# Spreading the matrix memory's output norm from four rows instead of twelve columns

## The chip, the cores and the metric

The kernel runs on one core of one Trainium2 chip. TensorE multiplies (PE in the profile, its weight loads PEld), VectorE (DVE) and ScalarE (ACT) do the elementwise work, GpSimd (POOL) starts some DMAs and does a little arithmetic, and SyncE (SP) starts the weight loads. The metric is the device time of one execution in microseconds. The kernel before takes 1542.36 us, the median of three runs that lie between 1541.53 and 1542.65 us.

## The reference, cut to what matters

One layer of a hybrid decoder is computed for a prompt of 256 tokens and 8 single-token samples, 264 tokens in all. Two groups of heads share one input projection, and their outputs go side by side into one output projection:

```
xn = rmsnorm(x, g_mix)
z = xn @ w_in
h_rg = RG-LRU scan;  y_rg = rmsnorm(h_rg * gelu(z[rg gate]), g_rg_out)         # 1024 channels
num = ...                                                                     # (token, 4 heads, 256)
den = maximum(abs(den), exp(-m_t));  h = num / den
h_ml = rmsnorm(h, g_ml_out)                                                   # per head, over 256
y_ml = h_ml * sigmoid(z[output gate])                                         # 1024 channels
x = x + concatenate([y_rg, y_ml]) @ w_out
x = x + cross_attention(rmsnorm(x));  x = x + swiglu(rmsnorm(x));  y = rmsnorm(x, g_final)
```

The change is about the factor of `h_ml`: one number for each of 264 tokens and 4 heads, which multiplies the 256 channels of that head. It joins the division by `den` and the norm's inverse root.

## The kernel before, in words

Activations lie transposed: 128 channels on the partitions, 264 tokens along the row. A matrix product is a sequence of *steps*, one for each block of 128 output channels, and a step is a run of up to 16 *chunks* of 128 input channels. To keep float32 precision, weights and activations are split into a high and a low half, and each chunk takes three products of one pass each (`mm3`, in the profile `mm<-B,W`); so a step of 16 chunks is 48 products. The steps touched here are, in this order, the eight RG gate blocks (25 to 32), the eight output-gate blocks (33 to 40, called o0 to o7 below), and the sixteen blocks of `w_out` (41 to 56, called out0, out1, ...). SyncE loads the weights (`raw`); for each half block ACT makes the high half and DVE the low half (`W<-raw`, `W<-raw,W`). A step's result is taken out of PSUM one step later ("evacuated"), on DVE first: for o0 to o7 it is multiplied by `rstd` into a temporary (`t<-mm,rstd`), goes through a sigmoid on ACT, is multiplied by the normed memory output (`t<-t,B`) and is split into the high and low half that `w_out` reads.

Beside the steps run *side works*, Python generators that are advanced after each step. The order in which all of it stands on each engine is not the order in which the code is written: a planner places every instruction by a timeline of its own when the kernel is built, and it is fixed from then on. Every engine takes its instructions strictly in that order.

Three pieces matter.

- `ml_norm` (line 850), the one that is changed. It sums the squares of each head over its 256 channels with `sums` (three products against a column of ones in each head, `ax<-ones,B`, for three blocks of 128 tokens; the third holds the 8 samples). The sums stand as 12 columns, 4 heads by 3 token blocks. DVE makes of them the 12 columns `f`, by an inverse root with three Newton steps (`c<-c`). `spread` (line 359) then turns a column back into a row that is the same on all partitions: the column, repeated 128 times, is the stationary operand, and the identity moves through. It takes three float32 products in each head (128, 128 and 8 columns), and each float32 product is two instructions on PE. DVE multiplies the head's two blocks by the row in PSUM (`B<-B,ax`).
- `later` and `drip` (lines 282 and 287): `sums` of one head are pinned behind a chunk of the running step. With `after=3` the next head's sums come four chunks later, with `after=1` two chunks later; the first head has 1 in both.
- `rg_out` (line 585) makes the RG group's half of what `w_out` reads. Its inverse root is `rstd_wide` (line 384): two one-pass products against ones (`ax<-B,ones_r`) and then twelve DVE instructions over the whole row, each of which needs the one before (`B<-ax`, `B<-B`, `lt<-B`, and three times `B<-lt`, `B<-B`, `lt<-B,lt`). With its result, the tile `lt`, DVE multiplies the eight blocks (`B<-B,lt`), and ACT and DVE split each into high and low (`B<-B,vecs` on ACT, `B<-B,vecs,B` on DVE). The first eight chunks of every `w_out` step read these blocks (`ry`, line 1037), so out0 cannot begin without the first.

```
def ry(c):
    return st["yrg"](c) if c < 8 else st["yml"](c - 8)
```

Buffers of the kind `B` are 26, handed out in turn; PSUM has four banks for the steps (`mm`) and four for all else (`ax`). `ident_r` is a 4 by 4 identity in the one-pass type, and is already used before for two products in each head that spread four rows (line 709: `sel = ident_r[:, h: h + 1].to_broadcast([4, P])`).

Of the kernel before, what the change touches and what calls it, by code (L numbers as in the profile page):

```python
# [10 lines left out]
F32 = mybir.dt.float32  # L11
F32R = mybir.dt.float32r
I32 = mybir.dt.int32
AF = mybir.ActivationFunctionType
# [3 lines left out]
P = 128  # L18
D = 2048
KC = D // P  # L20
T = 256
NS = 8
N = T + NS
# [67 lines left out]
def layer_kernel(ctx: ExitStack, tc, xT, memT, vec, wrg, w_in, w_out, w_q, w_k, w_v, w_o,  # L91
# [3 lines left out]
    act, dve, pe = Engine(nc.scalar, price_act), Engine(nc.vector, price_dve), Engine(nc.tensor, price_pe)  # L95
# [10 lines left out]
    def nm(s):  # L106
        uid[0] += 1
        return f"{s}_{uid[0]}"

    def view(t, shape, skip=0):  # L110
        v = t[:, skip: skip + int(np.prod(shape[1:]))]
        if len(shape) == 2:
            return v
        names = "abcd"[:len(shape) - 1]
        return v.rearrange(f"p ({' '.join(names)}) -> p {' '.join(names)}",
                           **{c: int(n) for c, n in zip(names[1:], shape[2:])})

    def B(shape, dt=F32, skip=0):
        return view(sb.tile([P, SLOT], dt, tag="B", bufs=NB, name=nm("B")), shape, skip)
# [162 lines left out]
    def later(*fs, after=0):  # L282
        k = [after, list(fs)]
        drips.append(k)
        return k
# [13 lines left out]
    def bank(tag="mm"):  # L299
        return psm.tile([P, 512], F32, tag=tag, bufs=4, name=nm(tag))  # L300
# [4 lines left out]
    ident = const.tile([P, P], F32, name="ident")  # L305
# [5 lines left out]
    ident_r = const.tile([4, H], F32R, name="ident_r")  # L311
# [20 lines left out]
    def ctile(w):  # L332
        t = sb.tile([P, 16], F32, tag="c", bufs=8, name=nm("c"))
        return t[:, :w]

    def rsqrt(v, y):

        w = v.shape[-1]
        i = ctile(w).bitcast(I32)
        dve.tensor_single_scalar(i, v.bitcast(I32), 1, op=OP.logical_shift_right)  # L340
        dve.tensor_scalar(y.bitcast(I32), i, -1.0, 1597463007.0, op0=OP.mult, op1=OP.add)
        t = ctile(w)
        for _ in range(3):
            dve.tensor_mul(t, y, y)
            dve.scalar_tensor_tensor(t, t, -0.5, v, op0=OP.mult, op1=OP.mult)
            dve.scalar_tensor_tensor(y, t, 1.5, y, op0=OP.add, op1=OP.mult)
# [5 lines left out]
    def token_sums(ps, acc, o=0, step=1):  # L352

        for j, w0 in enumerate(WIN if acc.shape[-1] == N else WIN[:2]):
            i = pe.matmul(ps[:, o + j * step: o + j * step + 1], acc[:, w0: w0 + P], ones[:, 0:1],
                          start=True, stop=True)
        return i

    def spread(ps, c, n=N):

        for j in range(2 if n == T else 3):
            lo, hi = (j * P, j * P + P) if j < 2 else (T, N)
            i = pe.matmul(ps[:, lo:hi], c[j].to_broadcast([P, P]), ident[:, P - (hi - lo):], start=True, stop=True)
        return i
# [39 lines left out]
    def sumsq(acc, x, first):  # L404
        if first:
            return act.activation(acc, x, AF.Square)
        s = tmp(x.shape[-1])
        i = act.activation(s, x, AF.Square)
        dve.tensor_add(acc, acc, s)
        return i  # L410
# [439 lines left out]
    def ml_norm():  # L850

        while not (ml["pg"].done and ml["sg"].done) or st["i"] < 33:
            yield STEP
        hh = hT["t"]
        a = B([P, H, N])
        for h in range(H):
            for vb in range(2):
                act.activation(hh(2 * h + vb)[:, T:N], nums[:, 2 * h + vb, :], AF.Copy)
            sumsq(a[:, h, :], hh(2 * h), True)
            sumsq(a[:, h, :], hh(2 * h + 1), False)  # L860
            yield 0.35
        yield STEP
        ps = bank("ax")
        r, v, f = ctile(12), ctile(12), ctile(12)

        def sums(h):
            i = token_sums(ps, a[:, h, :], 3 * h)
            if h == 0:
                dve.tensor_max(r.rearrange("p (h j) -> p j h", j=3), den.rearrange("p (h j) -> p j h", j=3),
                               emc.rearrange("p (j h) -> p j h", h=H))  # L870
                dve.reciprocal(r, r)
                dve.tensor_mul(v, r, r)
            if h == H - 1:
                dve.scalar_tensor_tensor(v, ps[:, 0:12], 1.0 / 256, v, op0=OP.mult, op1=OP.mult)
                dve.tensor_scalar(v, v, EPS, None, op0=OP.add)
                rsqrt(v, f)
                dve.tensor_mul(f, f, r)
            return i

        for h in range(H):  # L880
            k = later(lambda h=h: sums(h), after=3 if h else 1)
        while k[1]:
            yield STEP
        for h in range(H):
            ps = bank("ax")
            spread(ps, [f[:, 3 * h + j: 3 * h + j + 1] for j in range(3)])
            for vb in range(2):
                dve.tensor_mul(hh(2 * h + vb), hh(2 * h + vb), ps[:, :N])
            yield 0.7
            ml["nn"] = h + 1  # L890
# [511 lines left out]
    for i, (src, cols, pef, evf, need) in enumerate(steps):  # L1402
# [20 lines left out]
        ps = pef(i)  # L1423
# [13 lines left out]
        if i == 24:  # L1437
            ml["ng"] = side(ml_norm(), -1)
# [115 lines left out]
```

## Time and profile before

| what | before |
|---|---|
| median of three runs | 1542.36 us |
| the profiled execution's own time | 1543.04 us |
| its span, first to last instruction | 1541.3 us |
| PE busy | 1528.6 us, 99% of the span |
| DVE busy | 1061.2 us, 69% |
| ACT busy | 782.9 us, 51% |
| chain of work that ended last, share on PE | 98% |

A row of the timeline gives the start in us from the span's start, the length, the engine, the operation, the tiles as out<-in, and the count of instructions that it merges; in brackets stands how long the engine was idle before it and what ended the wait. A row of the chain of waits gives start, length, engine and tile. All instructions that pass the clock-keeping helper carry its line, L63, so they are told apart by their tiles. PE's rows overlap: a product of 264 columns takes some 0.28 us from start to end, while the next one starts 0.12 us after it.

### The profile page before, as it was taken

The page shows a single profiled execution, that of the slowest core. Times are in us where ns is not written, and L with a number is a line of the kernel's source. Part 1 is how long each engine was busy: PE and PEld are TensorE (multiplying, and loading weights), DVE is VectorE, ACT ScalarE, POOL GpSimd, SP SyncE. Part 2 cuts the span into 40 slices and gives each one's busy share as a digit, 9 for nine tenths or more (in the row PEclk, how much of TensorE's full clock was granted, in tenths as well). Part 3 has the DMA queues.
Part 4 walks back from the last instruction along what each step waited for, and adds up shares of the span by engine and source line. Part 5 has one row for each costly group of instructions (what it writes and reads, how often), then busy time and mean ns, then how long its engine had stood idle before and what let it go on. Part 6 is the DMA issues. An engine that isn't in the chain of part 4 may idle for free.

```text
span 1541.3 us, 30024 instructions
## 1 busy us (share of the span) xinstructions
PE 1528.6 (99%) x12056; PEld 1495.3 (97%) x12056; DVE 1061.2 (69%) x2012; ACT 782.9 (51%) x1233; POOL 126.9 (8%) x190
## 2 busy tenths in 40 slices
PE   8999999999999999999999999999999999999997
PEld 8999999999998888899999999999999999999997
DVE  7976887878798989966675555545555554555554
ACT  6455875655555666654444444334444433444463
POOL 0001120000133334310000000000000000000000
PEclk9999999999999999999999999999999999999999
DMA  7655886556789798856555555555555555555563
GB/s 287 198 169 179 300 306 219 183 183 233 258 317 332 258 350 294 273 167 199 179 188 181 183 187 180 187 181 184 186 181 187 181 187 183 181 189 179 164 176 114
DMA packets 92316, 326.00 MB, mean 212 GB/s; under 512 B 10801, under 2 KB 11233, under 8 KB 92177
## 3 DMA queue, kind: packets, MB, share of 16 engines
q1 hardware_dynamic: 76752, 270.40, 52.7%
q0 software_dynamic: 15136, 53.16, 9.7%
q8 instruction: 94, 1.54, 0.4%
q10 hardware_dynamic: 288, 0.53, 0.1%
q14 instruction: 46, 0.37, 0.1%
HBM read 312.78 MB, written 11.28 MB: 210 GB/s over the span
## 4 chain that ended last, share of the span: by engine, by line
PE 98%; DVE 1%; DMA 0%; ACT 0%; issue 0%; ACTq 0%; DVEq 0%
PE mm L63 93%; PE ax L63 5%; DVE B L63 0%; DMA xres<-xT 0%; DVE W L63 0%; ACT B L63 0%; DVE c L63 0%; DVE t L63 0%; ACTq L304 0%; DVE lt L63 0%; DVEq L1531 0%; ACT W L63 0%; ACT c L63 0%; ACT L63 0%; ACTq L63 0%
## 5 line engine op out<-in xcount | busy, mean ns | idle before, releaser
L63 PE MATMUL mm<-B,W 128*128 128x264 f32 (+2 forms) x11008 | 1363.2, 285 | 0.4 <-DVE W L63 0.4
L63 PEld LDWEIGHTS mm<-B,W 128*128 128x128 f32 x11008 | 1340.8, 188 | 12.1 <-DVE W L63 0.6
L63 ACT ACTIVATE W<-raw 128x1024 fp32r<-128x1024 f32 (+2 forms) x520 | 536.7, 1034 | 649.4 <-PE mm L63 445.5
L63 DVE TENSOR_TENSOR W<-raw,W 128x1024 fp32r<-128x1024 f32 (+2 forms) x520 | 620.2, 1195 | 353.7 <-ACT W L63 352.2
L63 PE MATMUL mm<-W,B 128*128 128x512 f32 x384 | 92.4, 395 | 0.0
L63 PEld LDWEIGHTS mm<-W,B 128*128 128x128 f32 x384 | 71.0, 188 | 16.1
L63 DVE TENSOR_TENSOR t<-mm,rstd 128x264 f32<-128x264 f32 x104 | 44.8, 432 | 44.1 <-PE mm L63 43.9
L1446 POOL TENSOR_TENSOR B<-B,rstd 128x264 f32<-128x264 f32 x4 | 2.8, 732 | 854.0 <-ACT rstd L63 854.0
L63 DVE TENSOR_TENSOR xres<-xres,mm 128x264 f32<-128x264 f32 (+1 forms) x81 | 34.2, 425 | 34.8 <-PE mm L63 34.7
L63 DVE SCALAR_TENSOR_TENSOR B<-B,dw 128x256 f32<-128x256 f32 x128 | 53.8, 475 | 1.8 <-ACT dw L63 1.7
L63 DVE SCALAR_TENSOR_TENSOR dw<-B,qsm,dw 128x256 f32<-128x256 f32 x96 | 51.4, 545 | 2.1 <-ACT dw L63 1.7
L63 PE MATMUL ax<-B,B 128*128 128x256 f32 (+3 forms) x288 | 48.2, 308 | 0.0
L1087 POOL TENSOR_TENSOR dr<-dw,dr 128x256 fp32r<-128x256 f32 x32 | 38.6, 1207 | 102.3 <-ACT dr L63 102.2
L63 PEld LDWEIGHTS ax<-B,B 128*128 128x128 f32 x288 | 40.9, 190 | 2.6
L63 ACT ACTIVATE B<-xres,vecs 128x264 fp32r<-128x264 f32 (+1 forms) x64 | 31.0, 502 | 2.0 <-DMA xres<-xT 1.9
L1076 POOL DMA_DIRECT2D B<-kcT x32 | 17.4, 543 | 134.9 <-DVE B L63 126.7
L63 ACT ACTIVATE dw<-B,qsm 128x256 f32<-128x256 f32 x32 | 16.3, 508 | 22.8 <-DVE B L63 8.9
L63 ACT ACTIVATE B<-t 128x264 fp32r<-128x264 f32 (+1 forms) x60 | 24.5, 408 | 4.5 <-DVE t L63 4.5
L63 ACT ACTIVATE t<-t 128x264 f32<-128x264 f32 (+1 forms) x61 | 24.7, 407 | 3.3 <-DVE t L63 3.3
L63 ACT ACTIVATE t<-xres 128x264 f32<-128x264 f32 (+2 forms) x46 | 18.7, 409 | 14.5 <-DVE xres L63 14.5
L63 DVE SCALAR_TENSOR_TENSOR B<-xres,vecs,B 128x264 fp32r<-128x264 f32 x48 | 22.3, 488 | 1.8 <-ACT B L63 1.8
L63 ACT ACTIVATE t<-B,B 128x128 f32<-128x128 f32 x64 | 19.9, 390 | 5.3 <-DMA B<-scr 5.3
(167 smaller groups left out, 657.2 us busy)
## 6 DMA issues: line engine op xcount, KB each, us to landing
raw<-w_gu SPq DMA_DIRECT2D x176, 512.0 KB, 3.6
raw<-w_d SPq DMA_DIRECT2D x80, 512.0 KB, 3.6
raw<-w_in SPq DMA_DIRECT2D x78, 512.0 KB, 4.5
raw<-w_out SPq DMA_DIRECT2D x32, 512.0 KB, 3.9
raw<-w_q SPq DMA_DIRECT2D x32, 512.0 KB, 5.3
B<-kcT POOLq DMA_DIRECT2D x32, 512.0 KB, 8.4
B<-vcT POOLq DMA_DIRECT2D x32, 512.0 KB, 9.7
raw<-w_k SPq DMA_DIRECT2D x32, 512.0 KB, 6.6
```

The costliest lines, as they stand in the source:

```text
L63: return f(*a, **k)
L1076: pool_e.dma_start(kc, kcT[h, b])
L1087: pool_e.tensor_sub(wr[:, 1], acc, wr[:, 0].bitcast(F32))
L1446: e.tensor_mul(st["y"](c), st["y"](c), r)
```

## The change

The twelve columns `f` are first turned into four rows, one for each head, with 264 tokens in a row: three float32 products whose stationary operand is the four heads' column of one token block and through which the identity moves (`turn`). ACT copies the rows as their high half, DVE takes the low half. A head's factor is then spread to all partitions by two one-pass products of 264 columns, whose stationary operand is a column of the 4 by 4 identity repeated 128 times. It takes one more PSUM bank (`fp`) and one more `B` buffer (`hl`). The sums of heads 1 to 3 come two chunks apart, instead of four.

```
+        fp = bank("ax")
+        hl = B([P, 2, N], F32R)[0:4]
+
+        def turn():
+            fj = f.rearrange("p (h j) -> p j h", j=3)
+            for j, w0 in enumerate((0, P, T)):
+                w = min(P, N - w0)
+                pe.matmul(fp[0:4, w0: w0 + w], fj[:, j, :], ident[:, P - w:], start=True, stop=True)
+            act.activation(hl[:, 0], fp[0:4, :N], AF.Copy)
+            dve.tensor_sub(hl[:, 1], fp[0:4, :N], hl[:, 0].bitcast(F32))
+
         for h in range(H):
-            k = later(lambda h=h: sums(h), after=3 if h else 1)
+            k = later(lambda h=h: sums(h), after=1)
         while k[1]:
             yield STEP
+        turn()
         for h in range(H):
             ps = bank("ax")
-            spread(ps, [f[:, 3 * h + j: 3 * h + j + 1] for j in range(3)])
+            sel = ident_r[:, h: h + 1].to_broadcast([4, P])
+            for k in range(2):
+                pe.matmul(ps[:, :N], sel, hl[:, k], start=k == 0, stop=k == 1)
             for vb in range(2):
                 dve.tensor_mul(hh(2 * h + vb), hh(2 * h + vb), ps[:, :N])
             yield 0.7
```

The planner orders the engines anew for this code. Three places are shown as they stand in a row in the two built kernels; the number behind a name is the buffer's.

On PE, where the factor is spread: first before, in step o4 (its bank is mm_3333), where c_3096 is `f` and ax_3192 to ax_3210 are the heads' banks.

```order
L63 MATMUL mm_3333<-B_139,W_3251 128x264
L63 MATMUL ax_3192<-ident,c_3096 128x128 x2
L63 MATMUL ax_3192<-ident,c_3096 128x8
L63 MATMUL ax_3198<-ident,c_3096 128x128 x2
L63 MATMUL ax_3198<-ident,c_3096 128x8
```

Four such groups stand there in one piece, five products into o4. Now the four rows are made (ax_3097) four products before the end of o3 (mm_3260):

```order
L63 MATMUL ax_3097<-ident,c_3096 4x128 x2
L63 MATMUL ax_3097<-ident,c_3096 4x8
L63 MATMUL mm_3260<-B_182,W_3107 128x264 x2
L63 MATMUL mm_3260<-B_183,W_3107 128x264
L63 MATMUL mm_3260<-B_182,W_3107 128x264
```

And they are spread 19 products into o4 (mm_3330); B_3098 holds their halves, and ax_3199 to ax_3214 are the heads' banks:

```order
L63 MATMUL ax_3199<-B_3098,ident_r 128x264
L63 MATMUL ax_3204<-B_3098,ident_r 128x264
L63 MATMUL ax_3209<-B_3098,ident_r 128x264
L63 MATMUL mm_3330<-B_163,W_3254 128x264
L63 MATMUL ax_3199<-B_3098,ident_r 128x264
L63 MATMUL ax_3204<-B_3098,ident_r 128x264
L63 MATMUL ax_3209<-B_3098,ident_r 128x264
L63 MATMUL ax_3214<-B_3098,ident_r 128x264 x2
```

One group of twelve float32 products became a group of three small ones and, 23 step products later, eight one-pass products in two groups. The RG group's two products against ones stood 24 step products into o4 and now stand 43 into it.

On DVE, from the end of the RG group's inverse root on: first before. lt_3097 is its result, t_3535 and t_3600 are the evacuations of o6 (mm_3482) and o7 (mm_3547), B_1699 and B_1704 the RG blocks, B_3312 their low halves.

```order
L63 SCALAR_TENSOR_TENSOR B_3099<-B_3099 128x264
L63 TENSOR_TENSOR t_3535<-mm_3482,rstd 128x264
L63 SCALAR_TENSOR_TENSOR lt_3097<-B_3099,lt_3097 128x264
L63 TENSOR_TENSOR B_1699<-B_1699,lt_3097 128x264 x4
L63 TENSOR_TENSOR W_3544<-raw_3462,W_3544 128x8x128
L63 TENSOR_TENSOR B_1704<-B_1704,lt_3097 128x264 x4
L63 TENSOR_TENSOR t_3535<-t_3535,B_2465 128x264
L63 SCALAR_TENSOR_TENSOR B_3312<-B_1699,vecs,B_3311 128x264 x4
L63 TENSOR_TENSOR W_3606<-raw_3531,W_3606 128x8x128
L63 SCALAR_TENSOR_TENSOR B_3391<-B_1704,vecs,B_3390 128x264 x2
L63 SCALAR_TENSOR_TENSOR B_3402<-t_3397,vecs,B_3401 128x264
L63 TENSOR_TENSOR t_3600<-mm_3547,rstd 128x264
```

And now, where lt_3099 is the result, t_3538 and t_3603 belong to o6 and o7 (mm_3550), and B_3315 is the low half:

```order
L63 SCALAR_TENSOR_TENSOR lt_3099<-B_3101,lt_3099 128x264
L63 TENSOR_TENSOR t_3538<-t_3538,B_2465 128x264
L63 TENSOR_TENSOR B_3101<-lt_3099 128x264
L63 SCALAR_TENSOR_TENSOR B_3101<-B_3101 128x264
L63 TENSOR_TENSOR W_3609<-raw_3531,W_3609 128x8x128
L63 SCALAR_TENSOR_TENSOR lt_3099<-B_3101,lt_3099 128x264
L63 TENSOR_TENSOR t_3603<-mm_3550,rstd 128x264
L63 TENSOR_TENSOR B_1699<-B_1699,lt_3099 128x264 x4
L63 TENSOR_TENSOR B_1704<-B_1704,lt_3099 128x264 x4
L63 TENSOR_TENSOR W_3612<-raw_3533,W_3612 128x8x128
L63 TENSOR_TENSOR t_3603<-t_3603,B_2465 128x264
L63 SCALAR_TENSOR_TENSOR B_3315<-B_1699,vecs,B_3314 128x264 x3
```

Before, the eight blocks are multiplied by the result, and four of them split, ahead of the evacuation of o7. Now the multiplications stand behind it.

On PE, where out0 (mm_3615) and out1 (mm_3688) begin, now; B_3314 and B_3315 are the high and low halves of the first four RG blocks:

```order
L63 MATMUL mm_3550<-B_182,W_3479 128x264
L63 MATMUL mm_3615<-B_3314,W_3544 128x264
L63 MATMUL mm_3688<-B_3314,W_3609 128x264
L63 MATMUL mm_3615<-B_3315,W_3544 128x264
L63 MATMUL mm_3615<-B_3314,W_3544 128x264 x2
L63 MATMUL mm_3688<-B_3315,W_3609 128x264
L63 MATMUL mm_3688<-B_3314,W_3609 128x264 x2
```

Before, the first three rows of out0 and out1 stood in the same order. In both, PE has two products to do with the first high half; the third needs the first low half.

## The prediction

> **What bounds the kernel now.** I read the page first. PE is busy almost throughout, and the chain that ended last runs along PE:
>
> ```profile
> span 1541.3 us, 30024 instructions
> PE 1528.6 (99%) x12056; PEld 1495.3 (97%) x12056; DVE 1061.2 (69%) x2012; ACT 782.9 (51%) x1233; POOL 126.9 (8%) x190
> L63 PE MATMUL mm<-B,W 128*128 128x264 f32 (+2 forms) x11008 | 1363.2, 285 | 0.4 <-DVE W L63 0.4
> ```
>
> So what PE does more or less is time, and so is any wait of PE. In 11008 step products PE waited 0.4 us in all; nothing later in the kernel has slack from which a loss could be repaid: the 12.7 us in which PE is idle lie at the start and behind its last product. Then I read the chain of waits in the stretch from the norm to `w_out`:
>
> ```profile
> 246.82 0.56 PE ax L63 x6
> 247.38 7.20 PE mm L63 x59
> 254.57 2.58 PE ax L63 x24
> 274.98 0.04 DVE B L63
> 279.22 1.70 DVE B L63 x4
> 280.92 1.15 DVE W L63
> 282.11 2.93 PE mm L63 x22
> ```
>
> The spread is 2.6 us of PE's path. But near 279 us the chain leaves PE and runs over DVE: that is the RG group's half of `w_out`'s input, and PE's one wait (0.42 us) stands at its end. Here DVE is just in time, which makes its order the second thing to look at.
>
> **The direct cost on PE.** The timeline of PE gives what is removed, and what a one-pass product costs:
>
> ```profile
> 253.81 0.76 PE L63 MATMUL mm<-B,W 128*128 128x264 f32 x5
> 254.41 2.74 PE L63 MATMUL ax<-ident,c 128*128 128x128 f32 x24
> 257.01 2.52 PE L63 MATMUL mm<-B,W 128*128 128x264 f32 x19
> 259.37 0.41 PE L63 MATMUL ax<-B,ones_r 128*128 128x264 f32 x2
> 259.61 0.64 PE L63 MATMUL mm<-B,W 128*128 128x264 f32 x4
> ```
>
> From start to start the 24 instructions take 257.01 - 254.41 = 2.60 us, 0.108 each; the five before them 0.12 each; the two against ones 0.24. The 19 behind take 2.36 us, 0.08 more than 19 x 0.12: the price of coming back to the steps. What is added has two near relatives:
>
> ```profile
> 126.95 0.47 PE L63 MATMUL ax<-ident,B 4*128 4x4 f32 x5
> 127.29 1.04 PE L63 MATMUL ax<-B,ident 4*128 4x16 f32 x8
> 147.91 0.50 PE L63 MATMUL ax<-B,ident_r 4*128 4x256 f32 x2
> 148.34 0.92 PE L63 MATMUL ax<-B,B 128*128 128x256 f32 x4
> ```
>
> The turn is six instructions. They lie between 0.067 us (0.34 / 5, a result of four partitions and four columns) and 0.108 us (the removed ones, with as many moving columns): 0.40 to 0.65 us; I take 0.55, since four of the six move 128 columns. The eight products are of the third row's kind, two in 0.43 us, 0.215 each, 1.72 us; if they ran like those against ones, at 0.12, 0.96 us. I take 1.72, as the row has the same operand of four partitions. There are three groups in place of one, so two more returns: 0.16 (0 to 0.32). The sum is -2.60 + 0.55 + 1.72 + 0.16 = -0.2 us, with bounds of -1.2 and +0.1. By TensorE: Matmul & The Clock Gate in the Trainium skill, section "Why this matters for your kernels", a product over 32 rows takes as long as one over 128, which would make it 0.12 each and the sum about -0.9; the third row above, at 0.215, does not agree.
>
> **What lies beside.** ACT's copy of four rows and DVE's subtraction (0.4 us each by rows of 264 elements below) stand between the turn and the spread, with 23 step products, 2.8 us, over them. The sums of squares are the same 24 instructions, only closer together; DVE's tiny column work starts earlier. The load queues and POOL issue what they did. A gain in any of this is hidden: what counts is when `w_out` can begin.
>
> **What the new order costs.** DVE takes its rows strictly in order. Before, the inverse root of the RG group ends just behind the evacuation of o6, and everything for out0 lies in the step that follows:
>
> ```profile
> 273.59 0.43 DVE L63 SCALAR_TENSOR_TENSOR B<-B 128x264 f32<-128x264 f32 x1
> 274.18 0.43 DVE L63 TENSOR_TENSOR t<-mm,rstd 128x264 f32<-128x264 f32 x1 [0.16 <-PE mm L63]
> 274.53 0.42 DVE L63 SCALAR_TENSOR_TENSOR lt<-B,lt 128x264 f32<-128x264 f32 x1
> 274.98 1.47 DVE L63 TENSOR_TENSOR B<-B,lt 128x264 f32<-128x264 f32 x4
> 276.37 1.22 DVE L63 TENSOR_TENSOR W<-raw,W 128x1024 fp32r<-128x1024 f32 x1
> 277.50 1.46 DVE L63 TENSOR_TENSOR B<-B,lt 128x264 f32<-128x264 f32 x4
> 278.88 0.43 DVE L63 TENSOR_TENSOR t<-t,B 128x264 f32<-128x264 f32 x1
> 279.22 1.70 DVE L63 SCALAR_TENSOR_TENSOR B<-B,vecs,B 128x264 fp32r<-128x264 f32 x4
> 280.84 1.22 DVE L63 TENSOR_TENSOR W<-raw,W 128x1024 fp32r<-128x1024 f32 x1
> ```
>
> The second row waits for PE: DVE reaches an evacuation before the step is done. In the new order the eight multiplications stand behind the next evacuation, that of o7, which cannot start before PE has done all that precedes `w_out`. The reason is in the order rows: the two products against ones come 19 step products later in o4, so the twelve dependent DVE instructions start behind other work and end one evacuation later.
>
> Let T be the moment at which PE could start out0. A product ends 0.285 us after its start and the next would start 0.12 after it, so the evacuation of o7 starts about T + 0.20. From there, in the new order and with the lengths above from start to start: the evacuation 0.35; eight multiplications at 1.39 / 4, 2.78; the weights' low half 1.13; the multiplication of o7's kind 0.34; the first low half 0.49 to its end. The first low half is there at T + 5.3. The first high half comes from ACT:
>
> ```profile
> 274.23 1.06 ACT L63 ACTIVATE W<-raw 128x1024 fp32r<-128x1024 f32 x1 [1.81 <-PE mm L63]
> 275.19 0.41 ACT L63 ACTIVATE t<-t 128x264 f32<-128x264 f32 x1
> 275.50 1.72 ACT L63 ACTIVATE B<-B,vecs 128x264 fp32r<-128x264 f32 x4
> ```
>
> In the new order the same three kinds follow each other behind o7, so it ends 0.20 + 1.27 + 0.50 after T, at T + 2.0. PE waits 2.0 us, does the two products that need only the high half, waits again until T + 5.3, 3.0 us, and then goes on; the fourth low half stands behind three of the other group, six places of 0.41 us behind the first, T + 7.7, against 17 products, T + 7.3: some 0.3 us more. That is 5.3 us of waiting. It takes the place of the 0.42 us before, which were for the weights of out1, now split ahead of o7's evacuation:
>
> ```profile
> 282.11 2.08 PE L63 MATMUL mm<-B,W 128*128 128x264 f32 x15 [0.42 <-DVE W L63]
> ```
>
> So the wait costs 5.3 - 0.4 = 4.9 us. Bounds: 4.4, if the smaller waits close up and DVE's hand-overs are free, and 5.3.
>
> **The clock behind the wait.** The windows show how PE's speed follows its work:
>
> ```profile
> 9.75:13.05 3.30, 3.30 (x16) 1.00 1.04 405
> 13.20:16.50 3.30, 3.30 (x29) 1.00 1.04 420
> 1532.00:1534.00 2.00, 1.27 (x12) 1.00 0.01 4
> 1534.00:1538.00 4.00, 0.00 (x0) 0.69 0.97 362
> 1538.00:1541.00 3.00, 0.00 (x0) 0.50 0.59 235
> ```
>
> (Columns: window, its length, PE busy and products, granted clock, DMA share, GB/s.) Until 13.1 us a product takes 0.22 us, then 0.12, though the column shows no throttle there. At the end PE has its last work before 1533.3, and the clock is halved at 1535.5, since a mean of 0.69 over 4 us is 1.5 us of full and 2.5 of half. So 2.2 us without work were enough. In the wait above PE works 0.24 us in 5.2, with one idle stretch of 3.0. I expect the clock to be halved there. What that costs is bounded by nothing below and, above, by the start, where PE needed this long at half speed before it got full speed:
>
> ```profile
> 8.00 5.26 PE L63 MATMUL ax<-B,W 128*128 128x264 f32 x20 [2.67 <-ACT B L63]
> 13.06 0.45 PE L63 MATMUL mm<-B,W 128*128 128x264 f32 x2
> ```
>
> That is 5.06 us, of which 1 - 0.12 / 0.22 is lost, 2.3 us. A slower PE also needs the late low halves later, which takes back the 0.3 us: 2.0 us.
>
> **The sum.** -0.2 + 4.9 + 2.0 = +6.7 us. The profiled execution took 1543.04 us with a span of 1541.3, 0.7 us above the median of 1542.36; on the median I predict 1549.1 us.
>
> **The rivals.**
> - *The clock stays up*: the same wait, but two idle stretches of 2.0 and 3.0 us, with work between, do not halve it. For it: at 254 us and elsewhere no such stretch exists, so the only row is that of the end, where the idle time went on. Then +4.7, 1547.1 us. The page named above says in the same section that idle gaps over about 3 us take the clock back, and in Part 1 that it takes a whole idle window of about 3.4 us; by that the clock stays here, and the time is this rival's.
> - *PE finds the halves ready* (the other side): if the RG chain catches up, so that the multiplications wait for nothing but their place, and the first low half is there at T, no wait is left, the 0.42 us goes too, and eight products at 0.12 save 1.2: 1540.7 us. It decides at the evacuation of o7: DVE would have to start it before o7 is done, against the bracket on the row at 274.18.
> - *Only the high half is late*: if the low half came within the 2 us of the first wait, 2.0 - 0.4 - 0.2 = +1.4, 1543.8 us. Against it stand nine DVE instructions between the first multiplication and the first low half, 3.9 us by the rows.
> - *The turn does not do what it says*: eight four-row products at 0.215 are no cheaper than the twelve of float32. This is inside the forecast, as -0.2 us.
>
> **How the numbers follow.** Forecast 0.55; the clock stays up 0.27; ready halves 0.05; only the high half late 0.08; a longer time at half clock, or a second halving, with 1551 us and more, 0.05. The forecast's own range is 1548 to 1550.2. For 8 in 10 the range must take in the second case down to 4.4 - 1.2 - 0, 1545.6 us, and goes up to 1551.0. A change of 0.2%, 3.1 us, is what a measurement of this kernel tells from none. Under 1539.3 I see only the second rival with an unseen gain, 0.02; within 0.2%, up to 1545.4, the two small-wait cases, 0.12; slower 0.86.
>
> **What would show it.** In the changed profile: the spread's eight products at 0.2 us each, and the three groups together about 2.4 us; DVE's row `B<-B,lt` behind the evacuation of o7; two idle stretches on PE's first `w_out` products, 2 and 3 us, released by ACT and by DVE; then about twenty products at 0.22 us and a granted clock of 0.5 for some 3 to 5 us; nothing later that differs. I am wrong if PE's idle time there is under 2 us, or if a difference arises behind 300 us.

## The result and the profile after

The changed kernel takes 1548.56 us, the median of six runs between 1547.83 and 1550.16; the kernel before, beside it, 1542.31 (1541.53 to 1542.65). The ratio is 1.004, with a 95% interval of 1.003 to 1.005: slower by some 6.2 us. The prediction was 1549.1. The profiled execution of the changed kernel took 1547.83 us, the lowest of its six, with a span of 1545.8.

The page of the changed kernel, its engines and the group of all step products:

```profile
span 1545.8 us, 30007 instructions
PE 1529.1 (99%) x12046; PEld 1494.6 (97%) x12046; DVE 1060.5 (69%) x2013; ACT 784.3 (51%) x1234; POOL 126.6 (8%) x190
L63 PE MATMUL mm<-B,W 128*128 128x264 f32 (+2 forms) x11008 | 1365.7, 285 | 4.6 <-DVE B L63 2.6
```

PE has 10 records less, and its step products waited 4.6 us where they had waited 0.4. The timeline of PE has the new groups and, at the end, the two waits:

```profile
245.75 6.27 PE L63 MATMUL mm<-B,W 128*128 128x264 f32 x51
251.94 0.64 PE L63 MATMUL ax<-ident,c 128*4 128x128 f32 x6
252.51 3.02 PE L63 MATMUL mm<-B,W 128*128 128x264 f32 x23
255.46 0.62 PE L63 MATMUL ax<-B,ident_r 4*128 4x264 f32 x3
256.01 0.39 PE L63 MATMUL mm<-B,W 128*128 128x264 f32 x1
256.33 0.87 PE L63 MATMUL ax<-B,ident_r 4*128 4x264 f32 x5
257.13 3.04 PE L63 MATMUL mm<-B,W 128*128 128x264 f32 x23
260.00 0.41 PE L63 MATMUL ax<-B,ones_r 128*128 128x264 f32 x2
260.24 18.01 PE L63 MATMUL mm<-B,W 128*128 128x264 f32 x149
280.17 0.59 PE L63 MATMUL mm<-B,W 128*128 128x264 f32 x2 [1.91 <-ACT B L63]
283.41 16.80 PE L63 MATMUL mm<-B,W 128*128 128x264 f32 x123 [2.65 <-DVE B L63]
```

On DVE the same stretch shows why: the evacuation of o7 comes first, and behind it the eight multiplications, the weights of the next step, one more multiplication, and only then the low halves.

```profile
277.70 0.43 DVE L63 SCALAR_TENSOR_TENSOR lt<-B,lt 128x264 f32<-128x264 f32 x1
278.29 0.43 DVE L63 TENSOR_TENSOR t<-mm,rstd 128x264 f32<-128x264 f32 x1 [0.16 <-PE mm L63]
278.64 2.83 DVE L63 TENSOR_TENSOR B<-B,lt 128x264 f32<-128x264 f32 x8
281.38 1.22 DVE L63 TENSOR_TENSOR W<-raw,W 128x1024 fp32r<-128x1024 f32 x1
282.52 0.43 DVE L63 TENSOR_TENSOR t<-t,B 128x264 f32<-128x264 f32 x1
282.86 1.30 DVE L63 SCALAR_TENSOR_TENSOR B<-B,vecs,B 128x264 fp32r<-128x264 f32 x3
```

On ACT the first high half is the third thing behind o7:

```profile
278.34 1.06 ACT L63 ACTIVATE W<-raw 128x1024 fp32r<-128x1024 f32 x1 [1.81 <-PE mm L63]
279.30 0.41 ACT L63 ACTIVATE t<-t 128x264 f32<-128x264 f32 x1
279.62 1.31 ACT L63 ACTIVATE B<-B,vecs 128x264 fp32r<-128x264 f32 x3
```

The clock, in windows cut where it changes (columns: window, its length, PE busy and products, granted clock, DMA share, GB/s):

```profile
277.03:280.45 3.42, 1.51 (x13) 1.00 0.60 207
280.45:283.86 3.41, 0.76 (x4) 0.50 0.14 42
283.86:287.27 3.41, 3.41 (x17) 0.50 0.37 138
287.27:290.69 3.42, 3.42 (x31) 1.00 0.00 0
```

It was half from 280.45 to 287.27, for 6.83 us. Up to 283.41 of that PE stood mostly in the second wait, which DVE ended and not PE, so this part cost nothing. In the third window PE was busy throughout and did 17 products; in the fourth, 31. The window ahead of the fall holds only the first wait: PE was busy for 1.51 us of it.

Whole times vary by a few us between executions, so a stretch is used in what follows: from the last evacuation before the first sums of squares (left as it was by the change) to a query evacuation in the cross attention. Before, and then after, on DVE:

```profile
239.76 0.43 DVE L63 TENSOR_TENSOR t<-mm,rstd 128x264 f32<-128x264 f32 x1 [0.43 <-PE mm L63]
408.80 0.42 DVE L63 TENSOR_TENSOR B<-mm,rstd 128x256 f32<-128x256 f32 x1 [0.51 <-PE mm L63]
```

```profile
238.31 0.43 DVE L63 TENSOR_TENSOR t<-mm,rstd 128x264 f32<-128x264 f32 x1 [0.43 <-PE mm L63]
413.34 0.42 DVE L63 TENSOR_TENSOR B<-mm,rstd 128x256 f32<-128x256 f32 x1 [0.51 <-PE mm L63]
```

That is 169.04 us before and 175.03 after, 5.99 more. From the second row to the end of the span it is 1132.5 us in both, so nothing later differs. What lies ahead of the first row was 1.45 us shorter in this execution of the changed kernel; that is chance, and the start of the program, where it arises, is shown below.

### The profile page after: what moved, and what is told of

It is laid out like the page before. It is cut to its first block, busy times and chain, and to the rows that moved or that the text cites. A ratio compares the mean times of both kernels' runs of the same rounds, so it can differ in the third digit from the quotient of the medians.

```text
span 1545.8 us, 30007 instructions
## 1 busy us (share of the span) xinstructions
PE 1529.1 (99%) x12046; PEld 1494.6 (97%) x12046; DVE 1060.5 (69%) x2013; ACT 784.3 (51%) x1234; POOL 126.6 (8%) x190
## 4 chain that ended last, share of the span: by engine, by line
PE 99%; DVE 1%; DMA 0%; ACT 0%; issue 0%; ACTq 0%; DVEq 0%
PE mm L63 93%; PE ax L63 5%; DVE B L63 0%; DMA xres<-xT 0%; ACT B L63 0%; DVE W L63 0%; DVE c L63 0%; ACTq L304 0%; DVE t L63 0%; DVEq L1545 0%; ACT W L63 0%; ACT c L63 0%; ACT L63 0%; ACTq L63 0%
```

## The experiments

The theory was this: the change's own work on PE costs next to nothing; the loss is that VectorE's multiplications of the RG blocks got behind the last evacuation, which makes PE wait at out0 and lose its clock. Two questions were put: is it the order of the RG half, or the new spread itself; and does the clock cost time of its own. The table has all versions together (us; the stretch is that of the profiled execution, with the same two rows).

| kernel | median | kernel before beside it | ratio, 95% interval | stretch | PE's waits at out0 |
|---|---|---|---|---|---|
| before | 1542.31 | | | 169.04 | 0.42 |
| the change | 1548.56 | 1542.31 | 1.004, 1.003 to 1.005 | 175.03 | 1.91 + 2.65 |
| the change, RG half two places earlier | 1541.95 | 1542.2 | 0.9998, 0.9989 to 1.0007 | 168.16 | none |
| before, RG half two places earlier | 1543.33 | 1542.2 | 1.0002, 0.9993 to 1.0011 | 168.27 | none |
| before, sums two chunks apart | 1541.92 | 1542.2 | 0.9997, 0.9988 to 1.0006 | 168.33 | none |
| the change, sums four chunks apart | 1549.86 | 1542.1 | 1.005, 1.0038 to 1.0062 | 176.13 | 4.05 + 1.46 |
| the change, 22 products as filler | 1546.71 | 1542.2 | 1.003, 1.002 to 1.0041 | 173.59 | none |
| the change, 9 products | 1548.8 | 1542.1 | 1.0045, 1.0033 to 1.0056 | 174.87 | 2.72 |
| the change, 13 products | 1547.87 | 1542.1 | 1.0038, 1.0025 to 1.0051 | 173.58 | 2.01 |
| the change, 17 products | 1547.27 | 1542.57 | 1.0027, 1.0016 to 1.0038 | 173.59 | 1.12 |
| the change again | 1549.79 | 1542.57 | 1.0048, 1.0034 to 1.0062 | 175.11 | 1.91 + 2.65 |

**The RG half earlier, with the change.**

```
-                st["rgout"] = side(rg_out(), 0)
+                st["rgout"] = side(rg_out(), -2)
```

> The changed kernel with the RG output work moved back by two places of the list, so that VectorE has the eight multiplications of the RG gate behind it before the last output-norm evacuations; the four-row spread is untouched. If the two waits at out0 are all of the loss (the theory): no wait at out0 above 0.2 us, no half clock in the middle, and 1541.3 to 1542.0 us, some 6.5 to 7 us below the changed kernel and level with the kernel before (1542.3) or up to 1 us below it. If the four-row spread itself is what costs (the rival: more PE work, switching between four-row and full products, buffers of the output norm held longer): no better than 1547. If other work that is moved aside by this is late in turn: a new wait of 1 us or more somewhere between o2 and o7.

DVE's timeline has the multiplications early, ahead of the evacuation in the third row and of all that follow:

```profile
250.22 0.77 DVE L63 TENSOR_TENSOR B<-B,lt 128x264 f32<-128x264 f32 x2
250.99 2.15 DVE L63 TENSOR_TENSOR B<-B,lt 128x264 f32<-128x264 f32 x6
255.56 0.42 DVE L63 TENSOR_TENSOR t<-mm,rstd 128x264 f32<-128x264 f32 x1
```

PE doesn't wait at out0, and the granted clock is whole there. The time is 1541.95 us, 6.6 below the changed kernel, with the four-row spread kept. So the spread is not what costs. No new wait of PE shows in the rest of the stretch either. The move does more than bring eight rows forward: the RG group's products against ones now stand between the first sums of squares, at 239.87 us, and the spread follows only at 269.45. Of all versions run this is the one to keep if the spread is wanted; it can't be told from the kernel before (0.9998).

**The same move without the change.** The same line, in the kernel before.

> The kernel before with the same move of the RG output work by two places; the old spread. Theory: only the 0.42 us wait of the kernel before at out0 goes, so 1541.8 to 1542.2 us. Beside the changed kernel with the same move it prices the change's own instructions on PE: the forecast says -0.2 us for the four-row spread; if the spread costs more than it removes, the changed kernel with the move is the slower of the two.

The median, 1543.33, missed the expected 1541.8 to 1542.2, but its interval holds no change. The stretch is sharper: 168.27 against 169.04, so the one wait of 0.42 us was worth 0.77. The starts of single products in the trace of before say where the rest is: where PE took up work again, the distance to the product before is 0.70 us, and to the next 0.225, where 0.12 is usual, 0.69 more in all. Beside the version above, the four-row spread itself is worth 168.16 - 168.27 = -0.11 us. That is hardly more than the 0.08 us by which the two stretches of the changed kernel in the table differ, so it shows that the spread costs nothing rather than what it saves.

**The sums alone.**

```
-            k = later(lambda h=h: sums(h), after=3 if h else 1)
+            k = later(lambda h=h: sums(h), after=1)
```

> The kernel before with one part of the change only: the sums of squares are taken two chunks apart (after=1), the spread is the old one. Theory: the order of VectorE's list at o6 and o7 decides, not the distance of the sums by itself; here the eight RG multiplications stand ahead of the evacuation of o6, so out0 doesn't wait: 1541.5 to 1542.3 us. If the longer distance of the sums is what makes the halves late in the change: a wait at out0 of 2 us or more and 1545 us or longer.

Here the planner put the eight multiplications ahead of o6's evacuation, the second row:

```profile
272.33 2.83 DVE L63 TENSOR_TENSOR B<-B,lt 128x264 f32<-128x264 f32 x8
275.08 0.43 DVE L63 TENSOR_TENSOR t<-mm,rstd 128x264 f32<-128x264 f32 x1
```

PE doesn't wait at out0, and the time is 1541.92 us. The distance of the sums by itself harms nothing.

**The rows alone.** The changed kernel, with the line above put back as it was.

> The changed kernel with the other half of the change undone: four rows and one-pass products stay, the sums of squares are taken four chunks apart as in the kernel before (after=3 for the second output head). The Newton steps of the last heads end later, so VectorE's eight RG multiplications stand even further behind. Theory: the waits at out0 add up to 6.5 to 7.5 us against 4.6 in the changed kernel, and with the half clock behind them the kernel takes 1549.5 to 1551.5 us. If the waits of the changed kernel come from the two-chunk distance: less wait than 4.6 us and 1546 or below.

The time, 1549.86, is in the expected range; the waits are not. They add up to 5.5 us. On DVE:

```profile
278.56 0.43 DVE L63 TENSOR_TENSOR t<-mm,rstd 128x264 f32<-128x264 f32 x1 [0.16 <-PE mm L63]
279.72 1.22 DVE L63 TENSOR_TENSOR W<-raw,W 128x1024 fp32r<-128x1024 f32 x1
280.86 0.42 DVE L63 SCALAR_TENSOR_TENSOR lt<-B,lt 128x264 f32<-128x264 f32 x1
281.55 2.83 DVE L63 TENSOR_TENSOR B<-B,lt 128x264 f32<-128x264 f32 x8
284.29 0.90 DVE L63 SCALAR_TENSOR_TENSOR B<-B,vecs,B 128x264 fp32r<-128x264 f32 x2
```

The multiplications begin 3.0 us behind the evacuation (0.35 in the change), but the weights' split is done ahead of them and not behind, so the first low half comes only some 1.2 us later, and the stretch is 1.1 us longer. So it is the four rows, by the order that the planner then made of the rest, that bring the loss; the closer sums make it a little smaller.

The traces bear out the reason that the prediction gave, the later place of the RG group's two products against ones. From the first row of the stretch to these products it is 17.3 us with the sums alone, 19.6 before, 21.7 in the change and 24.1 with the rows alone; the eight multiplications begin 33.8, 35.2, 40.3 and 43.0 us behind that row. What in the four rows makes the planner place them so (the products' new places, one more PSUM bank, one more buffer) was not tried.

**Filler in the wait.** The clock was tried by giving PE something to do. Products of a constant, whose result nothing uses, stand between o7 and out0. All else is in the order of the changed kernel, but for one pair of rows on DVE and one on ACT that change places some 10 us later, where PE doesn't wait. The edit is cut to its main lines:

```
+            if fill:
+                fb = bank("ax")
+                with tc.issue_after(st["m"].ins):
+                    for _ in range(fill):
+                        g = pe.matmul(fb[:, :P], ones, ones, start=True, stop=True)
...
+             need=("rgout",) if m == 0 else (), fill=22 if m == 0 else 0)
```

> The changed kernel with 22 float32 products of a constant (44 instructions, about 4.75 us at 0.108 us each) put on PE between the last output-norm group and out0; they are computed and not used, everything else stands in the same order. The RG halves come as late as in the changed kernel (T+2.0 and T+5.3), but PE has work while it waits for them. If the order of the late halves and the clock both cost what the forecast says: the waits shrink to about 0.5 us in all, the filler takes their place, no product near the start of the output projection takes 0.22 us, and the kernel takes about 1546.5 to 1547.2 us, 1.4 to 2 us less than the changed kernel's 1548.6. If the half clock is only a label in the records and costs nothing: 1548.6 again. If PE's products can't run beside VectorE's and ScalarE's work on the halves without holding it up: longer than 1549.

```profile
278.54 5.07 PE L63 MATMUL ax<-ones 128*128 128x128 f32 x44
283.37 0.88 PE L63 MATMUL mm<-B,W 128*128 128x264 f32 x3
```

With 4.8 us more of PE work than the changed kernel the time is 1546.71, 1.85 less, and the granted clock stays at 1.00 here. The stretch, 173.59 us, is 1.44 below that of the changed kernel: this is what the half clock costs.

**How much idle time it takes.** The same with 9, 13 and 17 products, and the changed kernel again beside the last.

> As the 22-product filler, but with 9 products (about 1.95 us): they cover the first wait, and the second one, about 2.8 to 3.0 us, stays. PE waits once instead of twice. If one gap of 3 us is enough to halve the clock: products of 0.22 us behind it for 3.4 or 6.8 us, and the same 1548.0 to 1549 as the changed kernel. If it takes the two gaps together (about 4.8 of 5.2 us idle): the clock stays whole and the kernel takes as long as with 22 products, 1546.5 to 1547.2 us.

> As the 22-product filler, but with 13 products (about 2.8 us): one wait of 2.0 to 2.4 us stays ahead of the first low half. If the clock follows the idle time in a window of about 3.4 us, whole windows only: no half clock, 1546.5 to 1547.2 us. If a wait of 2.2 us is enough, as the end of the program in the kernel before suggests: half clock behind it, about 1548 us.

> As the filler before, with 17 products (about 3.7 us): one gap of 1.1 to 1.4 us stays ahead of the first low half. The earlier traces show the clock changing on a grid of 3.41 us, halved after a stretch of the grid in which PE worked 0.44 of the time or less, and kept after one with 0.50 (9, 13 and 0 products of filler: 0.20, none, 0.44). If that is how it goes, a gap this short can take no stretch below 0.58, wherever the grid falls: no half clock in the middle in any execution, and 1546.2 to 1547.2 us, as with 22 products, without the times of 1547.7 to 1548.9 that four of the five executions with 13 products took. If any wait at out0 brings the half clock with it: 1548 again.

> The changed kernel itself, beside the 17-product filler on one chip: both theories have it at 1548 to 1549.5 us, with half clock behind out0 in every execution, because its two gaps (5.15 us with 0.25 us of work between them) always leave at least one stretch of the 3.41 us grid nearly empty. It gives the price of the half clock without a difference between chips: 1.4 to 2.0 us by the trace (16 products at 0.22 instead of 0.12 us, less what the gap lost anyway); under 0.5 us if the records of the clock mean nothing for the time.

The windows lie again on the grid on which the clock changes in each trace. With 9 products:

```profile
277.28:280.70 3.42, 3.42 (x31) 1.00 0.61 201
280.70:284.11 3.41, 0.69 (x5) 1.00 0.14 46
284.11:287.52 3.41, 3.41 (x18) 0.50 0.37 138
287.52:290.93 3.41, 3.41 (x30) 1.00 0.02 5
```

With 13, where the gap of 2.0 us was split between two windows:

```profile
278.71:282.13 3.42, 3.11 (x28) 1.00 0.48 158
282.13:285.54 3.41, 1.71 (x14) 1.00 0.44 147
285.54:288.95 3.41, 3.41 (x29) 1.00 0.04 14
```

With 17:

```profile
278.97:282.39 3.42, 2.30 (x20) 1.00 0.18 48
282.39:285.80 3.41, 3.41 (x29) 1.00 0.35 132
```

One gap of 2.7 us was enough to halve the clock, but for one window only, and it costs 174.87 - 173.59 = 1.28 us. In these traces the window decides: with PE busy for 0.69 or 1.51 us of it the next window came at half clock; with 1.71, 2.30 or more it didn't. Where the clock stayed whole, the stretch is 173.58 or 173.59 whether 13, 17 or 22 products stood there, because the late low half ends it, not PE.

The whole times were less clear. With 9 products the median, 1548.8, is in the range expected for a half clock. With 13, 1547.87 is near the 1548 expected for it too, though the profiled execution, at 1546.61 the shortest of the five, has none in the middle; the other four were not traced. The expectation on the single executions with 17 products was not borne out: no window in the middle can be empty enough there, and still the seven times lie between 1544.89 and 1549.87, wider than with 13, with a median of 1547.27 just above the range. The changed kernel beside it, 1549.79, came out 0.3 us above its range.

What varies is the start of the program. Here is its first long row on PE, with two windows of the grid around it, in the changed kernel:

```profile
7.88 3.87 PE L63 MATMUL ax<-B,W 128*128 128x264 f32 x19 [0.29 <-ACT W L63]
3.97:7.38 3.41, 0.98 (x8) 1.00 1.04 333
7.38:10.79 3.41, 3.12 (x14) 0.50 0.97 334
```

And in the kernel with 17 products:

```profile
7.77 2.58 PE L63 MATMUL ax<-B,W 128*128 128x264 f32 x19 [0.33 <-ACT W L63]
5.91:9.32 3.41, 1.93 (x13) 1.00 0.99 347
9.32:12.74 3.42, 3.42 (x31) 1.00 1.05 379
```

The same 19 products took 3.87 us, most of them at half clock, and 2.58 at full clock. It is the same rule: PE was busy for 0.98 us of one window and for 1.93 of the other, and the next came at half clock and at full. The row in front of the stretch starts at 236.83 us with 17 products, and at 238.31 and 240.04 in two executions of the changed kernel; in the second of these PE also got its first input some 0.7 us later than in the first. Behind the stretch all traces take 1132.5 us. So on whole times the price of the clock in the middle is known only roughly: 1549.79 against 1547.27 on one chip, 2.5 us, of which the stretch shows 1.52.

## Why the prediction was right, step by step

The stretch takes the sum apart, by differences between versions that add up to the whole by construction. Half clock: 175.03 - 173.59 = 1.44. The wait: 173.59 - 168.16 = 5.43. The spread: -0.11. The wait that was there before: -0.77. Together 5.99.

- **The late halves** were right in place and size. The evacuation of o7 begins at 278.29, so T is 278.1; the prediction had the first high half at T + 2.0 and the first low half at T + 5.3, and PE started on them at 280.17 and 283.41, T + 2.1 and T + 5.3. The waits of 1.91 and 2.65 us are released by ACT and DVE, as it said. The 0.3 us for a later fourth low half do not show in the changed kernel, since a slower PE wants it later. With 22 products as filler and a whole clock it does show: the product that needs it starts 0.25 us behind the one ahead and the next 0.23 behind that, where 0.12 is usual. So 5.3 stands against 5.43.
- **What it replaced was mis-sized.** The step "the wait costs 5.3 - 0.4" took the idle time of before for its price. It was worth 0.77, since the first two products behind a wait come late too: 5.43 - 0.77 = 4.7 us, where 4.9 was forecast.
- **The half clock** came where it was forecast and cost 1.44 instead of 2.0. Two steps to it were off. The first is the reason. The prediction took an idle stretch of 2.2 us, read at the end of before, as enough, and expected the stretch of 3.0 us to halve the clock. But the clock fell behind the window with the first wait, 1.91 us, and the kernel with 13 products kept its clock through a gap of 2.01 that was split between two windows: what counts here is how much work a window holds. The second is the bound from the start, 5.06 us at half speed: of the 6.83 us at half clock only those after 283.41, 3.86 us, had work in them. 3.86 x (1 - 0.12 / 0.22) is 1.75, and the 0.3 us of the low half come off. The prediction also read the start of before as not throttled. Its trace has no record of the clock ahead of 13.15 us, and the column shows 1.00 where there is none; the changed kernel's trace has 0.50 at the start, from 7.38 to 10.79.
- **The direct cost** was right in sum, -0.2 against -0.11, and wrong in its terms. A product from four rows does not take 0.215 us: in the row of five, the starts lie 0.225 us apart for the first pair and 0.12 for the others. By TensorE: Matmul & The Clock Gate in the Trainium skill, section "Why this matters for your kernels", a product over 32 rows takes as long as one over 128; the trace after agrees, and here one over 4 does too. The error was to divide a pair's time by two: the pair of before holds the change from one kind of product to the other. From start to start the three groups take 0.57 + 0.55 + 0.80 = 1.92 us, where 0.55 + 1.72 = 2.27 was reckoned. The step products about them lose 0.07 us before the first group, 0.19 between the first two, 0.20 at the single one and 0.11 behind the last, 0.57 in all, where three returns of 0.08, 0.24, were reckoned. The two errors cancel, 2.49 against 2.51, and that is luck.
- **The rivals.** "The clock stays up" fell by its condition: the clock was 0.50 with two idle stretches below 3 us. The Trainium skill, in TensorE: Matmul & The Clock Gate, had it that way; the measurement decides. Part 1 of TensorE: Matmul & The Clock Gate in the Trainium skill tells of a free-running window of 3413 ns. The grid seen here, 3.41 us, agrees, but a window with PE busy for 1.51 of 3.42 us was enough; it need not be idle. The filler that keeps the clock up came to 1546.71, near that rival's 1547.1. "Ready halves" is what the earlier RG half brings about: 1541.95 instead of 1540.7, because the eight products do not save the 1.2 us that it reckoned with.

Of what the prediction named as its signs, the order on DVE, the two idle stretches and their releasers are there, and nothing later differs. Within their groups the eight products came 0.12 us apart, but for the first pair, and not 0.2; the products at 0.22 were 17 and not about twenty; the clock was at 0.5 for 6.83 us and not for 3 to 5.

Two things are not settled. The first is whether the limit, between 1.51 and 1.71 us of work in a window, holds elsewhere; each side of it is one kernel. Behind the last products of the kernel with 13 as filler, twelve of 128 columns and four of 8, 1.87 us of busy time in a window did not keep the clock, so busy time is not quite what is measured. The second is the price at another place of the grid: in both profiled executions of the changed kernel the clock fell some 0.3 us behind the end of the first wait.

## What to carry to other kernels

When work is made shorter or moved on an engine that is full, look at the engine that is just in time, and at its order: here a spread that cost PE nothing (-0.11 us) moved eight multiplications behind one evacuation, and that cost 6 us. In these runs an idle time of PE had a price beyond itself, at its end (some 0.3 us for 0.42 of waiting) and in the clock (1.3 us for one gap of 2.7 us, 1.4 to 1.5 for gaps of 1.9 and 2.65 us), so a wait that can't be removed is better filled, or kept so short that more than half of each window of 3.41 us still holds work. Where whole times vary at the start, the distance between two rows that the edit leaves alone tells a tenth of a us.

## What the runs showed of the hardware

The clock changes on a grid of 3.41 us. Counted from the start of the program, the grid lay differently in each execution: in two of the changed kernel the clock was at half from 280.45 to 287.27 us and from 282.19 to 289.02, two windows each, and with a single gap of 2.7 us for one window. Against the work it lay alike in these two: the clock fell some 0.3 us behind the end of the first wait. Part 1 of TensorE: Matmul & The Clock Gate in the Trainium skill tells of such a window, which doesn't begin with the kernel; the traces agree. PE's work at half clock was 17 or 18 products in a full window, against 29 to 31. At the start one window at half clock made the first 19 products 1.3 us longer (3.87 against 2.58). And going from full products to those with four rows or four columns, and back, costs about 0.1 us each time (0.57 us for the six changes here, between the groups and the steps).
